# An S5 recurrence run as two halves, each half as two chains side by side, with eight GLU sums opened early

## The chip, the core and the metric

The kernel runs on one core of one Trainium2 chip. The metric is device time in microseconds of one execution. Smaller is faster. The engines named below are TensorE (PE: matmuls, with PEld for its weight loads), VectorE (DVE), ScalarE (ACT), GpSimd (POOL), and SyncE (SP), whose queue issues nearly all DMAs.

## What is computed

The reference runs a sequence of 256 tokens of width 2048 through two attention layers (the first block), and then through a second block, whose mixer is a bidirectional S5 state-space layer with a gated linear unit, followed by a squared-ReLU MLP. Everything is float32. The part that matters here, cut:

```
def s5_scan(u, lam_bar, b_bar, s0, reverse):           # per group of 16 channels, 64 complex states
    bu = einsum('btgh,gph->btgp', u, b_bar)
    bu = bu.at[:, first].add(lam_bar * s0)
    return associative_scan(s[t] = lam_bar * s[t-1] + bu[t])

def s5_mixer(h_ctx, h_lat, ...):                       # 128 groups, both directions
    y = u_lat * d
    for direction in range(2):
        st_lat = s5_scan(u_lat, lam_bar, b_bar, s_ctx_final, reverse)
        y = y + einsum('btgp,ghp->btgh', st_lat, c_mat).real
    z = gelu(y)
    a, g = split(z @ w_glu, 2)                         # w_glu is 2048 x 4096
    return a * sigmoid(g)

def second_block(x, ...):
    x = x + gt1 * rmsnorm(s5_mixer(modulate(rmsnorm(x))))
    x = x + gt2 * rmsnorm(square(relu(modulate(rmsnorm(x)) @ w1)) @ w2)
```

## The kernel before

Activations lie transposed: 16 tiles of 128 features by 256 tokens. Every large product streams its weights from memory as column tiles of 2048 x 128. A column tile comes in two halves of 512 KB (`_split`, DMA on SP's queue into the `raw` pool). ACT casts each half to a rounded high part (L130) and DVE, now and then POOL, subtracts that from it for a low part (L131). `mm_t` then makes 48 matmuls of 128x128 by 128x256 for one column tile: 16 steps of the contraction, each with high by high (L156), high by low (L157) and low by high (L158), into one bank of the PSUM pool `pj`, which has four banks. Beside the stream, small chunks of the modulation vectors' matrix-vector products (`bg`) are worked off. A chunk loads 1 MB (`graw`), and its product is two DVE multiply-adds (L230) or PE matmuls (L215).

The S5 mixer (`s5_mix`) cuts the sequence into 64 chunks of 4 tokens and turns the recurrence into one over 63 chunk borders. The 128 groups are 8 blocks of 16. For each block, inputs are normalised, transposed and multiplied into the chunk increments, which ACT and DVE write into a state tile `S` (L1388). Then `scan` runs 63 steps, each of three instructions: a complex product in one multiply (L1405), and two adds (L1406, L1407). A step needs the result of the step before. For each block there follows an output part. ACT copies the state into `sn`, one half of it reversed (L1458, L1459); PE makes the output `y` from the inputs (L1433) and from `sn` (L1464); GELU follows on ACT, with POOL's (L1484) or DVE's (L1478) multiplications in between; PE transposes (`zt`, L1495); and ACT writes the high part of `z` (L1499) and either a half-scaled copy, from which POOL subtracts (L1502, L1503), or DVE subtracts directly (L1505).

How the blocks are dealt out stands in a few constants. `SEGS = (2, 2, 2, 1, 1)` makes five segments of blocks with a state tile each. Segment 1 (32 groups) is scanned by POOL, the others by DVE. `SCANS = ((0,), (2,), (3, 4))` gives the DVE calls of `scan`, so segment 0 is a single chain of 32 groups, segment 2 another one, and the two last are written side by side. `ORDER` sets the order of the output parts. `POOL_V` says for which blocks POOL does the GELU multiplications. `BG_M` and `BG_B` say how many `bg` chunks are put ahead of the recurrence and behind each output part.

After the eight output parts, the GLU loop walks over 16 column pairs, `pa` and `pg` (32 column tiles, 1536 matmuls). The contraction runs in the order `kts`, in which the blocks are finished. Sums over the features (L363) run beside it, and the row sums (L373) end it. Then comes the MLP.

The order of the instructions on each engine is set by the scheduler of the framework, which plans the program with a timeline of its own. `issue_after` holds an instruction behind another in this order only, without a wait on the chip.

Of the kernel before, what the change touches and what calls it, by code (L numbers as in the profile page):

```python
# [43 lines left out]
NV = len(VEC)  # L44
SEGS = (2, 2, 2, 1, 1)
SCAN_POOL = (1,)
ORDER = (0, 2, 1, 3, 4)
SCANS = ((0,), (2,), (3, 4))
SLOT = (0, 0, 1, 0, 1)
P_START = ("pe",)  # L50
# [21 lines left out]
JOBS = ("m0", "m02", "mk", "m1", "mc", "m12", "m22", "m24", "m25")  # L72
DVE_W = 1
DVE_V = 1
POOL_V = tuple(range(7))
BG_M = 4
BG_B = 2
TL = True
# [28 lines left out]
class K:  # L107
# [40 lines left out]

    def mm_t(self, a, order=range(KT)):

        H, L = self.weights()
        ps = self.pj.tile([128, T], F32, name="pj", tag="pj")
        for kt in order:
            h, l = H[kt // 8][:, kt % 8], L[kt // 8][:, kt % 8]
            aH, aL = a(kt)
            self.nc.tensor.matmul(ps, h, aH, start=kt == order[0], stop=False)  # L156
            self.nc.tensor.matmul(ps, h, aL, start=False, stop=False)  # L157
            self.nc.tensor.matmul(ps, l, aH, start=False, stop=kt == order[-1])  # L158
        return ps
# [535 lines left out]
    def run(self):  # L695
        tc, I = self.tc, self.I
        from contextlib import ExitStack
        with ExitStack() as es:
# [53 lines left out]
            self.stream_init(items)  # L752
            self.limit = 160

# [582 lines left out]
    def s5_mix(self):  # L1337
        nc, V = self.nc, self.V
        v = nc.vector
# [24 lines left out]
        for k, r in enumerate(segs):  # L1364
            for b in r:
# [14 lines left out]
                uc = [self.sq.tile([64, 4, 2, 64], F32, name="uc", tag="sq") for _ in range(2)]  # L1380
                self.to_chunks(us, ub[b % 2], U[:, b], uc, k < DVE_W)
                for q in range(2):
# [4 lines left out]
                    def evac(ri, ps):  # L1387
                        (v.tensor_copy if ri and k < DVE_W else nc.scalar.copy)(  # L1388
                            S[k][:, n0:n0 + 8, ri, 1:64], ps[:, :, 0:63])
# [3 lines left out]

        def scan(e, *ks):

            a = []
            for n, k in enumerate(ks):
                G, g = 16 * len(segs[k]), 16 * segs[k].start
                o = 512 if k in SCAN_POOL else 800 + 240 * SLOT[k]
                a.append((S[k], view(AB, 4 * g, [[4, G], [2, 2], [1, 2]]), G,  # L1400
                          st[:, o:o + 4 * G].rearrange("p (n q r) -> p n q r", q=2, r=2),
                          st[:, o + 4 * G:o + 6 * G].rearrange("p (n r) -> p n r", r=2)))
# [33 lines left out]

        blocks = [b for k in ORDER for b in segs[k]]
        nxt = within(blocks[0])
        self.bg(BG_M)
        for k in SCAN_POOL:  # L1440
            scan(nc.gpsimd, k)
        for n, b in enumerate(blocks):
            k = seg[b]
            r = segs[k]
            for ks in SCANS:
                if b == r.start and k == ks[0]:
                    scan(v, *ks)
            if n == PF_N:
# [40 lines left out]
            if b == r.start:  # L1489
                zR[k] = self.sp.tile([128, 2 * len(r), 2, T], F32R, name=f"z{k}", tag=f"S{k}")  # L1490
            for s in range(2):
                rows = slice(64 * s, 64 * s + 64)
# [36 lines left out]
        for j in range(KT):  # L1529
            pa = self.mm_t(z_, kts)  # L1530
            af = self.tmp("ga")
# [6 lines left out]
            nc.scalar.activation(xq, x[:, j], AF.Square)  # L1538
            pg = self.mm_t(z_, kts)
            t = self.tmp("gg")  # L1540
# [115 lines left out]
def _layout(i):  # L1656
# [36 lines left out]
    o["b_out"] = _cols(a["b_w_out"][0])  # L1693
    o["glu"] = _cols(a["s5_w_glu_2"][0])
    o["mlp_in"] = _cols(a["w_mlp_in_2"][0])
    o["mlp_out"] = np.stack([_cols(a["w_mlp_out_2"][0, q * 2048:(q + 1) * 2048]) for q in range(4)])
# [32 lines left out]
```

## Time and profile before

| | |
|---|---|
| median of 3 runs | 2579.72 us (2577.77 to 2581.68) |
| profiled execution, its time | 2582.58 us |
| its span | 2580.7 us |
| PE busy | 2374.7 us (92%) |
| DVE busy | 1806.7 us (70%) |
| ACT busy | 1255.4 us (49%) |
| POOL busy | 211.5 us (8%) |
| moved by DMA | 644.66 MB |

Matmul durations overlap in the trace, since TensorE pipelines them. The spacing of their starts is what they cost. A busy share over the whole span mixes stages with different limits, so the stages are read one by one: the stretch in which the recurrence runs on DVE, and the GLU behind it, in which PE is busy throughout.

### The profile page before, as it was taken

What the parts mean: (1) busy time and instruction counts of PE and PEld (TensorE: products, weight loads), DVE (VectorE), ACT (ScalarE), POOL (GpSimd) and SP (SyncE); (2) the same over time, 40 slices, a digit from 0 to 9 for tenths busy, and PEclk for the clock granted to TensorE, in tenths of its full rate; (3) what the DMA queues carried; (4) which work ended last, traced back from release to release, by engine and by line L of the source; (5) the groups of instructions that cost most, each with busy time, mean ns of one, the idle gap of its engine ahead of it and who ended that gap; (6) DMA issues with size and microseconds to landing.
All of it is one profiled execution on the core that took longest, in us unless ns stands there. A gap on an engine that the chain in (4) does not pass through costs nothing.

```text
span 2580.7 us, 48360 instructions
## 1 busy us (share of the span) xinstructions
PE 2374.7 (92%) x18950; PEld 2054.5 (80%) x18950; DVE 1806.7 (70%) x3351; ACT 1255.4 (49%) x2178; POOL 211.5 (8%) x432
## 2 busy tenths in 40 slices
PE   5699999999899999999998634999799999999997
PEld 1299999999688888889986424999688888888885
DVE  3287778878775565788877999876765565665655
ACT  1455554454365555766654335544544443443442
POOL 0000000000011110000000754000000000000000
PEclk7599999999889999999998766999899999999998
DMA  9999999878869998888876634897366666666662
GB/s 322 343 341 324 326 323 339 311 259 321 263 237 337 325 334 296 281 269 272 276 237 213 208 108 138 320 316 263 113 188 190 190 190 186 186 187 191 190 185 93
DMA packets 203316, 644.66 MB, mean 250 GB/s; under 512 B 41008, under 2 KB 49456, under 8 KB 202704
## 3 DMA queue, kind: packets, MB, share of 16 engines
q1 hardware_dynamic: 195616, 620.47, 71.7%
q0 software_dynamic: 7472, 21.11, 2.1%
q8 instruction: 148, 2.42, 0.4%
q14 instruction: 80, 0.66, 0.1%
HBM read 613.71 MB, written 25.69 MB: 248 GB/s over the span
## 4 chain that ended last, share of the span: by engine, by line
PE 82%; DVE 11%; DMA 4%; ACT 2%; issue 1%; SPq 0%; DVEq 0%; POOL 0%; ACTq 0%
PE pj L169 18%; PE pj L156 12%; PE pj L157 12%; PE pj L158 12%; PE pj L170 9%; DMA graw<-in_w_mod 3%; PE g L215 3%; DVE scan_t L1406 3%; PE pjv L193 3%; PE pjv L194 2%; DVE scan_t L1405 2%; PE pjv L195 2%; DVE S L1407 2%; PE inc L690 1%; PE st L363 1%
## 5 line engine op out<-in xcount | busy, mean ns | idle before, releaser
L131 DVE TENSOR_TENSOR wl<-w,wh 128x1024 fp32r<-128x1024 f32 x638 | 778.4, 1224 | 471.8 <-ACT wh L130 462.3
L130 ACT CAST wh<-w 128x1024 fp32r<-128x1024 f32 x640 | 665.6, 1048 | 699.6 <-PE pj L169 280.6
L169 PE MATMUL pj<-h,wh 128*128 128x512 f32 x1024 | 363.3, 400 | 6.1 <-DVE h L413 4.3
L169 PE MATMUL pj<-d,wh 128*128 128x512 f32 x1024 | 358.6, 396 | 0.0
L170 PE MATMUL pj<-h,wl 128*128 128x256 f32 x1024 | 287.5, 281 | 1.1 <-DVE wl L131 1.1
L230 DVE SCALAR_TENSOR_TENSOR gacc<-graw,csilu,gacc 128x1024 f32<-128x1024 f32 x207 | 265.1, 1281 | 32.7 <-DMA graw<-in_w_mod 23.3
L170 PE MATMUL pj<-d,wl 128*128 128x256 f32 x1024 | 284.8, 279 | 0.0
L169 PEld LDWEIGHTS pj<-h,wh 128*128 128x128 f32 x1024 | 194.1, 190 | 54.6 <-issue 3.9
L169 PEld LDWEIGHTS pj<-d,wh 128*128 128x128 f32 x1024 | 191.9, 188 | 47.4 <-PE pj L170 1.7
L156 PE MATMUL pj<-hH,wh 128*128 128x256 f32 x768 | 221.4, 289 | 5.4 <-ACT hH L412 4.0
L158 PE MATMUL pj<-hH,wl 128*128 128x256 f32 x768 | 221.3, 289 | 0.5 <-DVE wl L131 0.5
L157 PE MATMUL pj<-hL,wh 128*128 128x256 f32 x768 | 221.0, 288 | 0.0
L215 PE MATMUL g<-graw,czc 128*32 128x256 f32 x1776 | 170.2, 467 | 53.0 <-DMA graw<-in_w_mod 50.0
L170 PEld LDWEIGHTS pj<-h,wl 128*128 128x128 f32 x1024 | 194.8, 190 | 1.5 <-DVE wl L131 1.5
L170 PEld LDWEIGHTS pj<-d,wl 128*128 128x128 f32 x1024 | 192.8, 188 | 0.4
L156 PEld LDWEIGHTS pj<-hH,wh 128*128 128x128 f32 x768 | 148.7, 194 | 9.0 <-ACT hH L412 4.1
L215 PEld LDWEIGHTS g<-graw,czc 128*32 128x32 f32 x1776 | 46.8, 119 | 132.7 <-DMA graw<-in_w_mod 107.9
L158 PEld LDWEIGHTS pj<-hH,wl 128*128 128x128 f32 x768 | 148.5, 194 | 4.5 <-issue 3.7
L157 PEld LDWEIGHTS pj<-hL,wh 128*128 128x128 f32 x768 | 148.7, 194 | 3.8 <-issue 3.7
L158 PE MATMUL pj<-z,wl 128*128 128x256 f32 x512 | 145.6, 285 | 2.9 <-POOL wl L131 2.7
L156 PE MATMUL pj<-z,wh 128*128 128x256 f32 x512 | 147.3, 289 | 1.0 <-ACT wh L130 1.0
L250 POOL TENSOR_TENSOR m<-gs,vecs 128x4 f32<-128x4 f32 x48 | 19.4, 428 | 1567.3 <-ACT gs L247 1567.3
(473 smaller groups left out, 5494.3 us busy)
## 6 DMA issues: line engine op xcount, KB each, us to landing
graw<-in_w_mod SPq DMA_DIRECT2D x384, 512.0 KB, 5.8
w<-in_mlp_in SPq DMA_DIRECT2D x128, 512.0 KB, 4.5
w<-in_mlp_out SPq DMA_DIRECT2D x128, 512.0 KB, 4.3
w<-in_a_in SPq DMA_DIRECT2D x96, 512.0 KB, 6.5
graw<-in_w_kvmod SPq DMA_DIRECT2D x64, 512.0 KB, 6.6
w<-in_b_in SPq DMA_DIRECT2D x64, 512.0 KB, 5.8
w<-in_glu SPq DMA_DIRECT2D x64, 512.0 KB, 5.4
w<-in_a_v SPq DMA_DIRECT2D x32, 512.0 KB, 5.6
```

The costliest lines, as they stand in the source:

```text
L130: nc.scalar.copy(h, src)
L131: (eng or (nc.gpsimd if next(self.spl) else nc.vector)).tensor_sub(l, src, h)
L156: self.nc.tensor.matmul(ps, h, aH, start=kt == order[0], stop=False)
L157: self.nc.tensor.matmul(ps, h, aL, start=False, stop=False)
L158: self.nc.tensor.matmul(ps, l, aH, start=False, stop=kt == order[-1])
L169: self.nc.tensor.matmul(ps, h, view(aH, 0, [[T, 2], [1, T]]), start=kt == order[0], stop=False)
L170: self.nc.tensor.matmul(ps[:, 0], l, aH, start=False, stop=kt == order[-1])
L193: self.nc.tensor.matmul(ps[:, i], aH[:, s], h, start=half == 0 and i == 0 and k == 0, stop=False)
L194: self.nc.tensor.matmul(ps[:, i], aH[:, s], l, start=False, stop=False)
L215: nc.tensor.matmul(st["g"][32 * q:32 * q + 32], self.cz[c][:, ch * 2 + s], raw[s][:, q * 256:q * 256 + 256], start=st["n"] == 0, stop=ch = ...
L230: nc.vector.scalar_tensor_tensor(acc, raw[s], cc, acc, op0=MUL, op1=ADD)
L1406: e.tensor_add(u, t[:, :, 0], s[:, :, :, c + 1])
```

## The change

The recurrence is cut into two halves of four blocks, each with one state tile. Both are scanned on DVE. Each half is written as two chains of 32 groups side by side: two multiplies, two adds, two adds per step. The second half's scan is put behind the first half's in the order. POOL scans nothing any more.

While the second half is scanned, the first eight contraction steps of eight GLU column tiles (`KO_J = 4` pairs, the blocks 0 to 3) are summed with weights that aren't split: one float32 matmul of 128x128 by 128x256 in place of three (`ko`, 64 of them), in the four `pj` banks. Their weights come from a new input `glu0`, a second copy of that part of the GLU matrix made on the host, in eight loads of 512 KB. For these eight column tiles the stream then skips the first half of the weights (`second_only`), with its cast and subtraction, and their `mm_t` makes 24 matmuls in place of 48.

Three constants of the output parts move work between engines: POOL does the GELU multiplications of the first five blocks only (before, seven), and DVE makes half of the `sn` copies of the last three (before, of the last). Of the `bg` chunks, 12 come ahead of the recurrence and none behind the output parts; before, there were 4 and 10. `DVE_W` is now compared with the block and not with the segment, which names the same two blocks.

```diff
-SEGS = (2, 2, 2, 1, 1)
-SCAN_POOL = (1,)
-ORDER = (0, 2, 1, 3, 4)
-SCANS = ((0,), (2,), (3, 4))
+SEGS = (4, 4)
+KO_J = 4
+KO_K = 8
-DVE_W = 1
-DVE_V = 1
-POOL_V = tuple(range(7))
-BG_M = 4
-BG_B = 2
+DVE_W = 2
+DVE_V = 3
+POOL_V = tuple(range(5))
+BG_M = 12
+BG_B = 0
...
         for i in range(2):
+            if i == 0 and j in self.second_only:
+                H.append(None)
+                L.append(None)
+                continue
...
-    def mm_t(self, a, order=range(KT)):
+    def mm_t(self, a, order=range(KT), ps=None, last=True):
...
-        def scan(e, *ks):
+        def scan(k):
             a = []
-            for n, k in enumerate(ks):
-                G, g = 16 * len(segs[k]), 16 * segs[k].start
+            G = 8 * len(segs[k])
+            for h in range(2):
+                g = 16 * segs[k].start + G * h
...
             for c in range(63):
-                for s, ab, G, t, u in a:
-                    e.tensor_mul(t, view(s, c, [[128, G], [64, 2], [0, 2]]), ab)
-                    e.tensor_add(u, t[:, :, 0], s[:, :, :, c + 1])
-                    e.tensor_add(s[:, :, :, c + 1], u, t[:, :, 1])
+                for s, ab, t, u in a:
+                    v.tensor_mul(t, view(s, c, [[128, G], [64, 2], [0, 2]]), ab)
+                for s, ab, t, u in a:
+                    v.tensor_add(u, t[:, :, 0], s[:, :, :, c + 1])
+                for s, ab, t, u in a:
+                    last = v.tensor_add(s[:, :, :, c + 1], u, t[:, :, 1])
...
+        def open_sums(kt, z):
+            w = self.raw.tile([128, 2 * KO_J, 128], F32, name="wko", tag="raw")
+            nc.sync.dma_start(w.rearrange("p j c -> p (j c)"), I["glu0"][kt])
+            for j in range(KO_J):
+                if kt == 0:
+                    ko.append(self.pj.tile([128, 2, T], F32, name="ko", tag="pj"))
+                for i in range(2):
+                    nc.tensor.matmul(ko[j][:, i], w[:, 2 * j + i], z, start=kt == 0 and i == 0, stop=False)
...
+            if n == 0:
+                with self.tc.issue_after(scan(0)):
+                    scan(1)
...
+                    if 2 * b + s < KO_K:
+                        late.append((2 * b + s, zh))
...
+            for kt, zh in late:
+                open_sums(kt, zh)
...
-            pa = self.mm_t(z_, kts)
+            if j < KO_J:
+                pa, pg = [self.mm_t(z_, kts[KO_K:], ko[j][:, i], i == 1) for i in range(2)]
+            else:
+                pa = self.mm_t(z_, kts)
```

How the scheduler places this is shown at three places. In the rows, the number behind a name tells buffers apart, and the lines of the changed kernel are its own (L1415, L1417 and L1419 are the three instructions of a step there).

The first place is DVE where a second chain joins. Before, `S_16015` is segment 0 (blocks 0 and 1) and `S_16017` segment 2 (blocks 4 and 5):

```order
L1405 TENSOR_TENSOR scan_t<-S_16015,scan_t 128x128
L1406 TENSOR_TENSOR scan_t<-scan_t,S_16015 128x64
L1407 TENSOR_TENSOR S_16015<-scan_t 128x64
L1405 TENSOR_TENSOR scan_t<-S_16015,scan_t 128x128
L1406 TENSOR_TENSOR scan_t<-scan_t,S_16017 128x64
L1406 TENSOR_TENSOR scan_t<-scan_t,S_16015 128x64
L1407 TENSOR_TENSOR S_16017<-scan_t 128x64
L1407 TENSOR_TENSOR S_16015<-scan_t 128x64
```

In the changed kernel, where `S_16015` is the first half (blocks 0 to 3), both chains write into it:

```order
L1419 TENSOR_TENSOR S_16015<-scan_t 128x64
L1415 TENSOR_TENSOR scan_t<-S_16015,scan_t 128x128
L1417 TENSOR_TENSOR scan_t<-scan_t,S_16015 128x64
L1419 TENSOR_TENSOR S_16015<-scan_t 128x64
L1415 TENSOR_TENSOR scan_t<-S_16015,scan_t 128x128
L1417 TENSOR_TENSOR scan_t<-scan_t,S_16015 128x64 x2
L1419 TENSOR_TENSOR S_16015<-scan_t 128x64 x2
L1415 TENSOR_TENSOR scan_t<-S_16015,scan_t 128x128 x2
```

Before, the partner was segment 2; now it is the other chain of the first half. It joins after 12 single steps of the first chain, and 12 single steps of the partner are left at the end of the half. Behind them every step of the second half is a pair, so that there are 51 pair steps, 12 single steps and 63 pair steps after the joining. This is the border of the halves on DVE, with `S_16016` the second half:

```order
L1415 TENSOR_TENSOR scan_t<-S_16015,scan_t 128x128
L1417 TENSOR_TENSOR scan_t<-scan_t,S_16015 128x64
L1419 TENSOR_TENSOR S_16015<-scan_t 128x64
L1415 TENSOR_TENSOR scan_t<-S_16016,scan_t 128x128 x2
L1417 TENSOR_TENSOR scan_t<-scan_t,S_16016 128x64 x2
L1419 TENSOR_TENSOR S_16016<-scan_t 128x64 x2
```

No other work of DVE stands between the two halves.

The second place is PE during the recurrence. Before, the last two output parts and the start of the GLU (L156 to L158) read so; `y` is an output sum, `zt` a transpose:

```order
L1464 MATMUL y_17709<-vl,sn 64x4x16 x32
L215 MATMUL g<-graw,czc_156 32x256 x12
L1495 MATMUL zt<-idn,zb 128x64 x8
L1433 MATMUL y_17800<-ml,U 64x4x16 x16
L1495 MATMUL zt<-idn,zb 128x64 x8
L1433 MATMUL y_17890<-ml,U 64x4x16 x16
L1464 MATMUL y_17800<-vl,sn 64x4x16 x32
L1464 MATMUL y_17890<-vl,sn 64x4x16 x32
L156 MATMUL pj<-z_17273,wh_0_18442 128x256
```

In the changed kernel, this is what PE has between the output parts of the first half:

```order
L1487 MATMUL y_17802<-vl,sn 64x4x16 x32
L1461 MATMUL ko<-zh,wko 128x256 x16
L1519 MATMUL zt<-idn,zb 128x64 x8
L1446 MATMUL y_17912<-ml,U 64x4x16 x16
L1487 MATMUL y_17912<-vl,sn 64x4x16 x4
L1461 MATMUL ko<-zh,wko 128x256 x16
L1519 MATMUL zt<-idn,zb 128x64 x8
L1487 MATMUL y_17912<-vl,sn 64x4x16 x20
L1461 MATMUL ko<-zh,wko 128x256 x16
```

The new matmuls stand in groups of 16 (two contraction steps of eight tiles) between the output parts, where the matrix-vector matmuls (L215) stood before.

The third place is DVE where the recurrence ends. Before, one block's output part is left behind it:

```order
L1405 TENSOR_TENSOR scan_t<-S_16019,scan_t 128x64
L1406 TENSOR_TENSOR scan_t<-scan_t,S_16019 128x32
L1407 TENSOR_TENSOR S_16019<-scan_t 128x32
L1459 COPY sn<-S_16019 64x1024 x2
L131 TENSOR_TENSOR wl_0_18604<-w_0_18601,wh_0_18603 128x1024
L131 TENSOR_TENSOR wl_1_18610<-w_1_18607,wh_1_18609 128x1024
L131 TENSOR_TENSOR wl_0_18624<-w_0_18621,wh_0_18623 128x1024
L1478 SCALAR_TENSOR_TENSOR y_18581<-y_18581,y_18461 128x512
```

In the changed kernel, four blocks' output parts are:

```order
L1415 TENSOR_TENSOR scan_t<-S_16016,scan_t 128x128 x2
L1417 TENSOR_TENSOR scan_t<-scan_t,S_16016 128x64 x2
L1419 TENSOR_TENSOR S_16016<-scan_t 128x64 x2
L1482 COPY sn<-S_16016 64x1024 x6
L1501 SCALAR_TENSOR_TENSOR y_18278<-y_18278,y_18132 128x512
L1501 SCALAR_TENSOR_TENSOR zb<-y_18278,y_18132 128x512
L1531 SCALAR_TENSOR_TENSOR z_18195<-zt,z_18195 128x256 x2
L135 TENSOR_TENSOR wl_1_18446<-w_1_18443,wh_1_18445 128x1024
L1501 SCALAR_TENSOR_TENSOR y_18367<-y_18367,y_18223 128x512
```

The `sn` copies and the GELU of three blocks have moved to DVE behind the scan. The ten other `sn` copies of this half, and its evacuations, stand on ACT behind the same point, with five casts (L130 before) among them. On PE, some 30 matmuls of GLU tiles stand ahead of the last transposes.

## Rows read from the trace of the kernel before

**Rows 1.** Windows, us; busy of PE, PEld, DVE, ACT, POOL; PEclk, DMA share, GB/s.

```profile
1539.60:1607.60 68.00, 34.62 (x564) 28.96 (x564) 65.45 (x304) 38.89 (x58) 26.03 (x34) 0.70 0.43 144
...
1612.30:1818.90 206.60, 203.36 (x1653) 187.32 (x1651) 152.27 (x153) 105.28 (x167) 9.48 (x10) 1.00 0.84 291
```

**Rows 2.** Waits over the whole span: total, times and longest, us.

```profile
ACT sn L1458 <- DVE S L1407: 87.0, 4, 53.4
...
POOL scan_t L1406 <- ACT S L1388: 36.0, 1, 36.0
```

**Rows 3.** Timeline of DVE, single chain: start us, duration us, instruction.

```profile
1417.62 0.29 DVE L1405 TENSOR_TENSOR scan_t<-S,scan_t 128x128 f32<-128x128 f32 x1
...
1418.55 0.29 DVE L1405 TENSOR_TENSOR scan_t<-S,scan_t 128x128 f32<-128x128 f32 x1
...
1425.25 0.35 DVE L1407 TENSOR_TENSOR S<-scan_t 128x64 f32<-128x64 f32 x1
```

**Rows 4.** Timeline of DVE, pair steps beside POOL's scan and without it.

```profile
1492.74 0.59 DVE L1407 TENSOR_TENSOR S<-scan_t 128x64 f32<-128x64 f32 x2
...
1494.36 0.59 DVE L1407 TENSOR_TENSOR S<-scan_t 128x64 f32<-128x64 f32 x2
...
1500.27 0.40 DVE L1407 TENSOR_TENSOR S<-scan_t 128x64 f32<-128x64 f32 x2
...
1501.33 0.39 DVE L1407 TENSOR_TENSOR S<-scan_t 128x64 f32<-128x64 f32 x2
```

**Rows 5.** Timelines of DVE and of POOL where POOL does an output part.

```profile
1589.89 0.23 DVE L1405 TENSOR_TENSOR scan_t<-S,scan_t 128x64 f32<-128x64 f32 x1
1590.15 0.22 DVE L1406 TENSOR_TENSOR scan_t<-scan_t,S 128x32 f32<-128x32 f32 x1
...
1590.65 1.23 DVE L1405 TENSOR_TENSOR scan_t<-S,scan_t 128x64 f32<-128x64 f32 x1
...
1594.66 0.67 DVE L1406 TENSOR_TENSOR scan_t<-scan_t,S 128x32 f32<-128x32 f32 x1
...
1590.53 1.26 POOL L1484 TENSOR_TENSOR y<-y,zb 128x512 f32<-128x512 f32 x1 [11.54 <-ACT y L1481]
...
1594.53 1.41 POOL L1503 TENSOR_TENSOR z<-zh,z 128x256 fp32r<-128x256 f32 x2
```

**Rows 6.** Groups of ACT's instructions, 1379 to 1609 us: busy us, mean ns.

```profile
L1458 ACT COPY sn<-S 64x1024 f32<-64x1024 f32 x16 | 16.6, 1045 | 90.9 <-DVE S L1407 87.0 <-POOL S L1407 3.6
...
L1481 ACT ACTIVATE y<-y 128x512 f32<-128x512 f32 x12 | 7.5, 629 | 0.2
...
L1499 ACT ACTIVATE z<-zt 128x256 fp32r<-128x256 f32 x12 | 4.7, 388 | 8.2 <-PE zt L1495 8.2
...
L130 ACT CAST wh<-w 128x1024 fp32r<-128x1024 f32 x2 | 2.1, 1036 | 0.0
```

**Rows 7.** Timeline of ACT: first and last instruction of two blocks' output parts.

```profile
1539.57 1.04 ACT L1458 COPY sn<-S 64x1024 f32<-64x1024 f32 x1 [14.14 <-DVE S L1407]
...
1558.28 0.41 ACT L1502 ACTIVATE zh<-zt 128x256 f32<-128x256 f32 x1
```

**Rows 8.** Windows inside the GLU and just behind it, columns as in Rows 1.

```profile
1630.00:1660.00 30.00, 30.00 (x238) 26.16 (x237) 26.18 (x27) 17.48 (x30) 1.60 (x2) 1.00 0.98 375
1700.00:1760.00 60.00, 60.00 (x504) 56.61 (x503) 45.01 (x45) 29.88 (x48) 1.44 (x2) 1.00 0.92 321
...
1825.00:1835.00 10.00, 6.32 (x21) 5.25 (x21) 8.76 (x23) 5.09 (x11) 0.00 (x0) 0.51 0.00 0
```

**Rows 9.** Timeline of PE: float32 transposes; the GLU's first matmul.

```profile
1389.15 1.92 PE L667 MATMUL o<-idn,u 128*64 128x128 f32 x8 [0.79 <-ACT u L1378]
...
1600.69 0.39 PE L156 MATMUL pj<-z,wh 128*128 128x256 f32 x1
```

**Rows 10.** The page: GLU weight loads (KB, us to landing), and matrix-vector multiply-adds.

```profile
L230 DVE SCALAR_TENSOR_TENSOR gacc<-graw,csilu,gacc 128x1024 f32<-128x1024 f32 x207 | 265.1, 1281 | 32.7 <-DMA graw<-in_w_mod 23.3
...
w<-in_glu SPq DMA_DIRECT2D x64, 512.0 KB, 5.4
```

More of the change, by code (lines that the diff above doesn't have):

```diff
@@ L44 @@
 NV = len(VEC)
-SEGS = (2, 2, 2, 1, 1)
-SCAN_POOL = (1,)
-ORDER = (0, 2, 1, 3, 4)
-SCANS = ((0,), (2,), (3, 4))
-SLOT = (0, 0, 1, 0, 1)
+SEGS = (4, 4)
+KO_J = 4
+KO_K = 8
 P_START = ("pe",)
@@ L147, in weights @@
         return self.ready.pop(j)
-    def mm_t(self, a, order=range(KT)):
+    def mm_t(self, a, order=range(KT), ps=None, last=True):
         H, L = self.weights()
-        ps = self.pj.tile([128, T], F32, name="pj", tag="pj")
+        opened = ps is not None
+        if not opened:
+            ps = self.pj.tile([128, T], F32, name="pj", tag="pj")
         for kt in order:
@@ L155, in mm_t @@
             aH, aL = a(kt)
-            self.nc.tensor.matmul(ps, h, aH, start=kt == order[0], stop=False)
+            self.nc.tensor.matmul(ps, h, aH, start=kt == order[0] and not opened, stop=False)
             self.nc.tensor.matmul(ps, h, aL, start=False, stop=False)
-            self.nc.tensor.matmul(ps, l, aH, start=False, stop=kt == order[-1])
+            self.nc.tensor.matmul(ps, l, aH, start=False, stop=kt == order[-1] and last)
         return ps
@@ L752, in run @@
             self.stream_init(items)
+            g0 = items.index(next(x for x in items if x.tensor is I["glu"].tensor))
+            self.second_only = set(range(g0, g0 + 2 * KO_J))
             self.limit = 160
@@ L1337, in s5_mix @@
     def s5_mix(self):
-        nc, V = self.nc, self.V
+        nc, V, I = self.nc, self.V, self.I
         v = nc.vector
@@ L1380, in s5_mix @@
                 uc = [self.sq.tile([64, 4, 2, 64], F32, name="uc", tag="sq") for _ in range(2)]
-                self.to_chunks(us, ub[b % 2], U[:, b], uc, k < DVE_W)
+                self.to_chunks(us, ub[b % 2], U[:, b], uc, b < DVE_W)
                 for q in range(2):
@@ L1387, in evac @@
                     def evac(ri, ps):
-                        (v.tensor_copy if ri and k < DVE_W else nc.scalar.copy)(
+                        (v.tensor_copy if ri and b < DVE_W else nc.scalar.copy)(
                             S[k][:, n0:n0 + 8, ri, 1:64], ps[:, :, 0:63])
@@ L1392, in s5_mix @@
             nc.scalar.copy(S[k][:, :, :, 0], self.s0[:, 16 * r.start:16 * r.stop])
-        def scan(e, *ks):
+        def scan(k):
             a = []
-            for n, k in enumerate(ks):
-                G, g = 16 * len(segs[k]), 16 * segs[k].start
-                o = 512 if k in SCAN_POOL else 800 + 240 * SLOT[k]
-                a.append((S[k], view(AB, 4 * g, [[4, G], [2, 2], [1, 2]]), G,
+            G = 8 * len(segs[k])
+            for h in range(2):
+                g = 16 * segs[k].start + G * h
+                o = 512 + 384 * k + 192 * h
+                a.append((S[k][:, G * h:G * h + G], view(AB, 4 * g, [[4, G], [2, 2], [1, 2]]),
                           st[:, o:o + 4 * G].rearrange("p (n q r) -> p n q r", q=2, r=2),
@@ L1403, in scan @@
             for c in range(63):
-                for s, ab, G, t, u in a:
-                    e.tensor_mul(t, view(s, c, [[128, G], [64, 2], [0, 2]]), ab)
-                    e.tensor_add(u, t[:, :, 0], s[:, :, :, c + 1])
-                    e.tensor_add(s[:, :, :, c + 1], u, t[:, :, 1])
+                for s, ab, t, u in a:
[4 more added lines that the diff above has]
+                    last = v.tensor_add(s[:, :, :, c + 1], u, t[:, :, 1])
+            return last.ins
         zR = {}
@@ L1435, in within @@
             return vt, y
-        blocks = [b for k in ORDER for b in segs[k]]
+        blocks = [b for r in segs for b in r]
+        ko = []
+        def open_sums(kt, z):
[6 more added lines that the diff above has]
+                    nc.tensor.matmul(ko[j][:, i], w[:, 2 * j + i], z, start=kt == 0 and i == 0, stop=False)
         nxt = within(blocks[0])
         self.bg(BG_M)
-        for k in SCAN_POOL:
-            scan(nc.gpsimd, k)
         for n, b in enumerate(blocks):
@@ L1444, in s5_mix @@
             r = segs[k]
-            for ks in SCANS:
-                if b == r.start and k == ks[0]:
-                    scan(v, *ks)
+            if n == 0:
+                with self.tc.issue_after(scan(0)):
+                    scan(1)
             if n == PF_N:
@@ L1490, in s5_mix @@
                 zR[k] = self.sp.tile([128, 2 * len(r), 2, T], F32R, name=f"z{k}", tag=f"S{k}")
+            late = []
             for s in range(2):
@@ L1538, in s5_mix @@
             nc.scalar.activation(xq, x[:, j], AF.Square)
-            pg = self.mm_t(z_, kts)
+            if j >= KO_J:
+                pg = self.mm_t(z_, kts)
             t = self.tmp("gg")
@@ L1694, in _layout @@
     o["glu"] = _cols(a["s5_w_glu_2"][0])
+    o["glu0"] = a["s5_w_glu_2"][0][:128 * KO_K].reshape(KO_K, 128, 2, 16, 128)[:, :, :, :KO_J].transpose(
+        0, 1, 3, 2, 4).reshape(KO_K, 128, 256 * KO_J)
     o["mlp_in"] = _cols(a["w_mlp_in_2"][0])
```

## The prediction

> **What bounds the kernel now.** I went from the stages to the single instructions. The windows [rows 1] show two stages that the change touches. In the last part of the recurrence, 1539.6 to 1607.6, PE is busy for 34.6 of 68 us and DVE for 65.5: DVE's steps set the pace, and PE has half its time free. In the GLU, 1612.3 to 1818.9, PE is busy for 203.4 of 206.6 us, and DVE (152.3) and ACT (105.3) are not full. So the first stage is worth what DVE's chain gets shorter, the second what PE has less to do. The waits [rows 2] agree: ACT's `sn` copies wait 87.0 us in four pieces for DVE's last step of a chain, and nothing of that length waits for ACT. All prices of steps come from the DVE timeline.
>
> A step of one chain of 32 groups takes 1418.55 - 1417.62 = 0.93 to 0.94 us for three instructions of 0.27 to 0.29 [rows 3]: each waits for the one before. Two chains side by side take 1494.36 - 1492.74 = 1.62 us per pair step while POOL scans, and 1501.33 - 1500.27 = 1.06 us when POOL is still [rows 4]. A pair thus costs little more than a single step, and far less than two (1.88).
>
> **The change, part by part.** (a) *The recurrence.* Up to 1425.2 nothing differs in the order on DVE: the first chain has made 12 single steps then [rows 3], and blocks 2 and 3 have just been written, since POOL's scan of them began there, after its wait of 36.0 us for their evacuation [rows 2]. From there the order of the changed kernel has 51 pair steps, 12 single steps and 63 pair steps, with nothing between the halves. POOL scans no more, so a pair step is priced at the clean 1.06; the contended 1.62 is its upper end. That gives 51 x 1.06 = 54.1, 12 x 0.94 = 11.3 and 63 x 1.06 = 66.8, together 132.2 us.
>
> (b) *POOL's output work beside the second half.* Its four output parts put 8 instructions of L1484 and 8 of L1503 on POOL. Where POOL begins an L1484 of 1.26 us, a DVE instruction takes 1.23 in place of 0.23, which is 1.0 more; beside the pair of L1503 (1.41 for two) one takes 0.67 in place of 0.22, some 0.46 more [rows 5]. 8 x 1.0 + 8 x 0.46 = 11.7 us. The lower end is 0 (POOL's instruction falls into a gap), the upper one the whole of POOL's time, 8 x 1.26 + 8 x 0.71 = 15.8. I take 11.7, what the DVE rows show. The Trainium skill, "SBUF — State Buffer", section "SBUF: two separate sides", says that a DVE instruction with two SBUF inputs and a GpSimd one that reads SBUF exclude each other for a whole instruction; by it the sum would be the upper end, 4 us more. The rows lie below that, since DVE has often begun first.
>
> The scan then ends at 1425.2 + 132.2 + 11.7 = 1569.1, against 1607.6 before: **-38.5 us**.
>
> (c) *The new matmuls.* 64 float32 matmuls of 128x128 by 256 columns don't occur before. Eight float32 transposes of 128 columns take 1.92 us [rows 9], 0.24 each, so 0.48 for 256 columns and 31 us for all; a rounded 256-column matmul takes 60.0 / 504 = 0.119 [rows 8], so 7.6 us is the low end. Either fits: in the 68 us window alone PE has 33 us idle [rows 1], and the second half of the scan lasts 78 us. I cost them at nothing. Without cover they would cost their 31. Their eight loads take 5.4 us each at most [rows 10], 43 us if each waited for the one before, also under 78; they stand in SP's queue ahead of the later `ml`, `vl` and GLU loads, and the four `pj` banks that they hold are wanted next by a GLU tile that follows their release. Zero, upper end 5.4 for one late load.
>
> (d) *The tail.* Before, one block's output part is left when the scan ends, and GLU matmuls resume 1612.3 - 1607.6 = 4.7 us later with work that doesn't need that block. Now four blocks are left, and GLU tiles have only the steps 8 to 15 to sum, all from these blocks. ACT's part of the tail, from the order: 10 `sn` copies, 5 casts, 10 evacuations and 11 GELU instructions. With [rows 6] that is 10 x 1.045 + 5 x 1.036 + 10 x 0.39 + 11 x 0.6 = 26.2 us. I add 2.3 for waits on PE's transposes (8.2 us are spread over 12 in [rows 6], so three or four such waits): 28.5. It costs 28.5 - 4.7 = **+23.8 us**. Low end 24 in all, no wait and hidden casts; high end two pairs of blocks as today, 1539.57 to 1558.69, 19.1 us each [rows 7], 38.2. The six `sn` copies, GELU multiplications and subtractions on DVE run beside ACT's; if ACT did the copies, that would be 6 x 1.045 more.
>
> (e) *The GLU.* Before, the first 12 of its 1536 matmuls run from 1600.69 on [rows 9], ahead of the scan's end, so 1524 remain. Now there are 1536 - 192 = 1344, of which some 30 stand before the last transposes in the order and run inside the tail. 1314 are left, 210 fewer: 210 x 0.119 = **-25.0 us** [rows 8]. The other work in that stage (row sums, gate chunks) stays.
>
> (f) *The clock.* PE runs little in the tail, and behind the GLU, where it is 63% busy, the granted clock is 0.51, the lower level [rows 8]. If the first 30 matmuls run at it, 3.6 us; if not, 0. I take **+2**.
>
> (g) *Edits at nothing.* Eight casts and eight subtractions fewer (ACT and DVE have room in the GLU). 12 chunks ahead of the recurrence and none behind, 14 before: two move into the GLU, four multiply-adds of 1.28 us [rows 10] on a DVE with 54 us idle there [rows 1]; uncovered 5.1.
>
> Sum: -38.5 + 23.8 - 25.0 + 2 = -37.7 us. Profiled: 2582.6 - 37.7 = 2544.9. The profiled execution lies 2.9 above the median of the runs, so the median becomes **2542**. The tail and the skipped matmuls cancel to within 1.2 us; the gain is that of the recurrence.
>
> **The rivals.** *A tail pair by pair.* PE and ACT do blocks 4 and 5 and then 6 and 7 with their waits, as the two-block parts before: 38.2 in place of 28.5, so 9.7 more, **2552**. For: those parts do take 19.1 us each. Against: the order has all `sn` copies first. Chance 0.17.
>
> *Eight light tiles starve.* A tile with 24 matmuls lasts 2.86 us, and asks for one half of weights and one 1 MB chunk, 1.57 MB, 4.2 us at the 375 GB/s of the densest window [rows 8]. Eight such tiles lose 8 x 1.34 = 10.7 us: **2553**. For: that window's DMA share is 0.98 already. Against: the order puts the eight half loads ahead of the chunks' loads on SP's queue. Chance 0.11.
>
> *Slower: pairs don't overlap on DVE.* If the two chains' instructions wait for each other, since both now write into one state tile, a pair step costs 2 x 0.94 = 1.88, and 114 of them cost 0.82 more each: +93.5, **2635**. The change is a loss from a pair step of 1.06 + 37.7 / 114 = 1.39 us on. For: the chains before had a tile each. Against: the measured pairs take 1.06, and even beside POOL's scan 1.62 [rows 4]; the order alternates the two with nothing between. The Trainium skill, "VectorE: DVE Perf Modes", section "The DRAIN you can't avoid", speaks for this rival: the next instruction waits for the pipe to empty, and leaving out semaphores doesn't skip that (though one that isn't held may begin earlier). By it the pair would cost two single steps; [rows 4] of this kernel disagree. Chance 0.05.
>
> *Better.* POOL's work falls into gaps, the tail is 24, the clock is not lost: 11.7 + 4.5 + 2 = 18 less at best, **2524**; half of it, 2533, is nearer. Chance of under 2530: 0.05. Several small costs that leave less than 5.2 us of gain: 0.02.
>
> **How the numbers follow.** The forecast has 0.60. Its own bounds are POOL's 15.8 (+4.1), the clock's 3.6 (+1.6), a late load of 5.4, and on the other side part of the 18: 2533 to 2552. The range takes in the two rivals of 2552 and 2553 with the forecast's own upper costs, and stops short of the others: **2530 to 2560**. What a measurement of this kernel can tell from no change is about 0.2%, 5.2 us. Faster by more: 0.60 + 0.17 + 0.11 + 0.05 = 0.93; within: 0.02; slower: 0.05.
>
> **What would show it.** In the profile of the changed kernel: 1.06 us from one second add of a pair to the same of the next in the second half, with POOL silent; the last step near 1569; DVE instructions stretched to 1.2 us only beside POOL's GELU multiplications; the 64 new matmuls between the transposes of the first four blocks, done before the scan ends; 28 us from the last step to the last high part of `z`; and from there some 182 us to the end of the GLU's matmuls, at a granted clock of 1.00. A pair step of 1.39 or more, PE waiting for weights in the first eight column tiles, or a tail near 38 would make it wrong, each by the amount above.

## The result, and the profile of the changed kernel

The changed kernel takes 2545.97 us (median of four runs, 2543.05 to 2548.22) against 2580.32 us for the kernel before (four runs): a ratio of 0.9867, with a 95% interval of 0.9850 to 0.9884. It is 34 us faster, where 38 were forecast, and its time lies inside the range. Its profiled execution has a span of 2546.4 us, 34.3 less than before.

The span can be cut at four points: the first add of the recurrence on DVE, its last add, the last high part of `z` on ACT, and the start of the row sums that end the GLU. Up to the last add and up to the last high part, the duration of that instruction is counted in. The kernel before differs in the third point: its last high part comes at 1624.0, when the GLU is running again, so there the tail ends where the GLU's matmuls resume, at 1612.3.

| us | before | forecast | changed |
|---|---|---|---|
| first add of the recurrence at | 1413.4 | 1413.4 | 1408.9 |
| recurrence, first add to last | 194.2 | 155.7 | 158.1 |
| from there until the GLU has PE to itself (the tail) | 4.7 | 28.5 | 31.9 |
| GLU, to its row sums | 206.5 | 183.5 | 183.5 |
| behind the GLU, to the end of the span | 761.8 | 761.8 | 764.0 |

These are the three stages in the windows of the changed kernel (columns as in [rows 1]):

```profile
1408.90:1567.00 158.10, 105.62 (x1268) 80.29 (x1266) 155.38 (x758) 61.22 (x119) 23.20 (x30) 0.80 0.57 181
1567.00:1598.90 31.90, 21.39 (x386) 20.17 (x387) 16.12 (x22) 23.63 (x37) 6.87 (x5) 0.72 0.47 149
1598.90:1782.40 183.50, 180.49 (x1448) 163.41 (x1446) 142.33 (x144) 91.80 (x148) 3.86 (x6) 0.99 0.89 312
```

DVE still fills the recurrence (155.4 of 158.1 us), PE still fills the GLU (180.5 of 183.5). Between them lies a stretch that hardly was there before, in which no engine is full: the tail. The waits of ACT answer to [rows 2]:

```profile
ACT sn L1481 <- DVE S L1419: 41.0, 3, 32.1
...
ACT z L1523 <- PE zt L1519: 18.7, 6, 7.6
```

The waits of ACT for a finished chain went from 87.0 to 41.0 us. The timeline of DVE in the changed kernel answers to [rows 3] and [rows 4]: first the pair joining, then the second adds of the last three steps, the last step whole.

```profile
1421.14 0.29 DVE L1415 TENSOR_TENSOR scan_t<-S,scan_t 128x128 f32<-128x128 f32 x1
1421.46 0.45 DVE L1417 TENSOR_TENSOR scan_t<-scan_t,S 128x64 f32<-128x64 f32 x2
...
1564.49 0.40 DVE L1419 TENSOR_TENSOR S<-scan_t 128x64 f32<-128x64 f32 x2
...
1565.55 0.40 DVE L1419 TENSOR_TENSOR S<-scan_t 128x64 f32<-128x64 f32 x2
...
1565.85 0.49 DVE L1415 TENSOR_TENSOR scan_t<-S,scan_t 128x128 f32<-128x128 f32 x2
1566.26 0.44 DVE L1417 TENSOR_TENSOR scan_t<-scan_t,S 128x64 f32<-128x64 f32 x2
1566.61 0.40 DVE L1419 TENSOR_TENSOR S<-scan_t 128x64 f32<-128x64 f32 x2
```

A pair step takes 1.06 us (from one row of L1419 to the next), as read before the change, although both chains now write into one state tile. The tail shows on POOL, DVE, PE and ACT (their timelines, one after the other):

```profile
1575.36 2.52 POOL L135 TENSOR_TENSOR wl<-w,wh 128x1024 fp32r<-128x1024 f32 x1 [30.77 <-issue]
1577.83 1.72 POOL L1507 TENSOR_TENSOR y<-y,zb 128x512 f32<-128x512 f32 x1
1581.72 1.26 POOL L1507 TENSOR_TENSOR zb<-y,zb 128x512 f32<-128x512 f32 x1 [2.17 <-ACT y L1504]
...
1574.97 0.69 DVE L1482 COPY sn<-S 64x1024 f32<-64x1024 f32 x1 [1.01 <-PE y L1487]
1575.99 2.45 DVE L1482 COPY sn<-S 64x1024 f32<-64x1024 f32 x1 [0.32 <-PE y L1487]
...
1583.04 0.77 PE L1519 MATMUL zt<-idn,zb 64*128 64x64 f32 x8 [7.16 <-POOL zb L1507]
...
1598.27 0.66 ACT L1523 ACTIVATE z<-zt 128x256 fp32r<-128x256 f32 x2 [1.39 <-PE zt L1519]
```

PE stands 7.16 us for POOL's second multiplication of block 4, and POOL began that block late, behind a weight subtraction of 2.52 us (L135). While it ran, a copy on DVE took 2.45 us, where the one before it took 0.69. That this is what makes the tail 31.9 us was the obvious reading, and the experiments don't bear it out.

### The profile page after: what moved, and what is told of

It is laid out like the page before. It is cut to its first block, busy times and chain, and to the rows that moved or that the text cites. A ratio compares the mean times of both kernels' runs of the same rounds, so it can differ in the third digit from the quotient of the medians.

```text
span 2546.4 us, 47968 instructions
## 1 busy us (share of the span) xinstructions
PE 2377.1 (93%) x18854; PEld 2051.9 (81%) x18854; DVE 1776.8 (70%) x3360; ACT 1239.5 (49%) x2153; POOL 118.8 (5%) x234
## 4 chain that ended last, share of the span: by engine, by line
PE 84%; DVE 9%; DMA 3%; ACT 2%; issue 1%; SPq 0%; POOL 0%; DVEq 0%; ACTq 0%; POOLq 0%
PE pj L176 18%; PE pj L163 12%; PE pj L164 12%; PE pj L165 12%; PE pj L177 9%; PE g L222 3%; PE pjv L200 3%; DMA graw<-in_w_mod 3%; PE pjv L201 2%; PE pjv L202 2%; DVE scan_t L1415 2%; DVE scan_t L1417 2%; DVE S L1419 2%; PE inc L697 2%; PE st L370 1%
## 5 line engine op out<-in xcount | busy, mean ns | idle before, releaser
L135 DVE TENSOR_TENSOR wl<-w,wh 128x1024 fp32r<-128x1024 f32 x631 | 770.0, 1224 | 465.2 <-ACT wh L134 457.2
L237 DVE SCALAR_TENSOR_TENSOR gacc<-graw,csilu,gacc 128x1024 f32<-128x1024 f32 x211 | 270.2, 1281 | 27.4 <-DMA graw<-in_w_mod 18.6
L163 PE MATMUL pj<-h1H,wh 128*128 128x256 f32 x512 | 147.1, 290 | 0.3 <-ACT ctx_ws L1323 0.2
L164 PE MATMUL pj<-h1L,wh 128*128 128x256 f32 x512 | 146.4, 287 | 0.0
L165 PE MATMUL pj<-h1H,wl 128*128 128x256 f32 x512 | 146.0, 286 | 0.0
```

The source lines that it names most:

```text
L163: self.nc.tensor.matmul(ps, h, aH, start=kt == order[0] and not opened, stop=False)
L237: nc.vector.scalar_tensor_tensor(acc, raw[s], cc, acc, op0=MUL, op1=ADD)
```

## The experiments

**The changed kernel again**, as a measure for the others.

> The changed kernel itself once more, as the measure for the runs beside it: 2543 to 2549 by its four runs so far. If the part behind the GLU (the MLP) takes 764 us in its profile again, that part is slower in this kernel; if 758 to 762 as in the other profiles, the 2 to 5 us were this execution's own.

It took 2546.71 us (2541.08 to 2549.19). Recurrence 158.0, tail 31.9, GLU 183.5: the same to 0.1 us. The first add comes at 1411.4, 2.5 later. Behind the GLU it took 760.1, so the 764.0 above are that execution's own; the twelve profiles of this study lie between 758 and 764 there. Runs of one kernel spread over 8 us, but these three stages repeat to a tenth, and so they are compared below wherever a few us matter.

**Without the early sums.**

```diff
-KO_J = 4
+KO_J = 0
...
-                    if 2 * b + s < KO_K:
+                    if KO_J and 2 * b + s < KO_K:
```

> The changed kernel without the early sums: all 32 GLU column tiles have 48 matmuls again, and the 64 unsplit matmuls with their eight loads are gone. Theory (the early sums are hidden behind the second half's recurrence, and each GLU matmul that they spare is worth its spacing): 192 x 0.119 = 22.8 us more than the changed kernel's 2546, of which up to 24 matmuls (2.9 us) can run before the tail: 2566 to 2569. Rival (the recurrence alone made the gain, and the shortened GLU tiles were limited by loads or casts, so that the spared matmuls gave nothing): 2546. Second rival (the early sums lengthen the recurrence or the tail by as much as they spare): 2546 as well, with the tail shorter than 32 us and the GLU longer by 23.

2565.73 us, 19 to 20 more. These rows are the last high part of `z` on ACT and the row sums on PE:

```profile
1602.59 0.38 ACT L1523 ACTIVATE z<-zt 128x256 fp32r<-128x256 f32 x1
...
1800.53 1.02 PE L380 MATMUL ysum<-sel_y,ysumt 128*128 128x4 f32 x4 [0.46 <-ACT ysumt L377]
```

The recurrence is as long as with the sums (157.6 us), so they cost it nothing. From its end to the row sums it is 233.9 us against 215.4, 18.5 more; 192 matmuls at 0.119 would be 22.8. Of the 4.3 between, 24 matmuls of one GLU tile (2.9) are hidden: they now run from 1574.9 to 1580.8, where PE otherwise waits in the tail. The last 1.4 I did not follow. Both rivals are out.

**The early sums twice.** Each matmul of L1461 is issued a second time; eight GLU tiles get the contribution of the blocks 0 to 3 doubled.

```diff
+                    nc.tensor.matmul(ko[j][:, i], w[:, 2 * j + i], z, start=False, stop=False)
```

> The changed kernel with each of the 64 early matmuls made twice, so that eight GLU tiles get the contribution of the blocks 0 to 3 doubled: 32 us more of TensorE work in the second half of the recurrence. Theory (these matmuls lie in TensorE's idle time beside VectorE's steps, 33 us of it in the second half's 78): 0 to 5 us more, 2546 to 2551, the few us from the output parts that are queued behind them on TensorE. Rival (the early sums aren't covered, they have cost their 32 us or a good part of it in the changed kernel too): 2560 to 2578.

2549.92 us, 3 to 4 more by the medians; by the stages it is 7. The sums keep PE busy for 58.0 us in place of 32.2, so the work added is 26 us and not the 32 expected, and 43.9 of the 58.0 lie ahead of the scan's end. The recurrence's second half with the doubled sums, and its tail:

```profile
1489.00:1564.20 75.20, 54.68 (x440) 47.71 (x440) 75.20 (x378) 17.32 (x32) 14.40 (x19) 0.84 0.28 86
1564.20:1605.20 41.00, 34.31 (x492) 30.89 (x493) 14.48 (x22) 25.57 (x42) 10.04 (x10) 0.93 0.46 152
```

Even so PE has 20 us idle beside DVE's steps. The tail is 9 us longer, since the last of the four blocks was finished only there (its sums begin at 1571.50, behind the scan's end at 1564.2). PE's part of that block, queued behind the doubled sums, was done at 1546.8, which still was in time. What held it is the order on ACT, where the block's last GELU step (L1505 here) stands behind two `sn` copies of the next block, and these wait for the scan's end:

```profile
1564.15 1.04 ACT L1482 COPY sn<-S 64x1024 f32<-64x1024 f32 x1 [13.67 <-DVE S L1419]
1565.20 1.04 ACT L1483 COPY sn<-S 64x1024 f32<-64x1024 f32 x1
1566.27 0.63 ACT L1505 ACTIVATE y<-y 128x512 f32<-128x512 f32 x1
```

The single sums are covered (the run without them shows it too), and what limited the cover here was not PE's idle time, but that an output part got behind the end of the recurrence in another engine's order.

**One wide chain per half.**

```diff
-            G = 8 * len(segs[k])
-            for h in range(2):
+            G = 16 * len(segs[k])
+            for h in range(1):
```

> The changed kernel with each half scanned as one chain of 64 groups in place of two of 32 side by side: half as many instructions, each twice as wide, each waiting for the one before. Theory (side by side, the second chain's instruction fills the time in which the first's result is awaited): from 0.75 us for a step of 16 groups and 0.94 for 32, a step of 64 should take about 1.32, against 1.07 for a pair. The first half then takes 63 x 1.32 = 83 us from 1421 on in place of 67, and the second 83 in place of 67: 33 us more, about 2579, all of the change's gain. Rival (a step costs its elements alone, however it is written): the same 1.07, 2546. Second rival (cost in proportion to the groups): 1.88 a step, 2646.

2570.43 us, 24 more. The timeline of DVE, one step:

```profile
1544.95 0.42 DVE L1415 TENSOR_TENSOR scan_t<-S,scan_t 128x256 f32<-128x256 f32 x1
1545.40 0.38 DVE L1417 TENSOR_TENSOR scan_t<-scan_t,S 128x128 f32<-128x128 f32 x1
1545.82 0.38 DVE L1419 TENSOR_TENSOR S<-scan_t 128x128 f32<-128x128 f32 x1
1546.24 0.42 DVE L1415 TENSOR_TENSOR scan_t<-S,scan_t 128x256 f32<-128x256 f32 x1
```

A wide step takes 1.29 us against 1.06 for a pair, with the same elements. In the wide step each instruction starts 0.03 to 0.04 us after the one before has ended; in a pair the rows of two instructions each (0.49, 0.44 and 0.40 in the last step shown above) add up to 1.33, more than the step. So two independent chains do overlap on DVE. Over the 114 pair steps that is worth 114 x 0.23 = 26 us, most of the change's gain. Another 12 x (1.29 - 0.94) = 4 come from something else: in the changed kernel the first chain makes 12 single steps while blocks 2 and 3 are prepared, for which the wide chain has to wait. The stages say 28.2 from the changed kernel's scan end to this one's. The step of 1.32 that I had extrapolated was too long by 0.03, 4 us over 126 steps.

**GpSimd quiet beside the recurrence.** GELU multiplications and subtractions of all blocks on DVE; the half-scaled copy on ACT stays for the early sums.

```diff
-POOL_V = tuple(range(5))
+POOL_V = ()
...
-                if n in POOL_V:
+                if 2 * b + s < KO_K:
...
-                    nc.gpsimd.tensor_sub(aL, zh, aH)
+                    v.tensor_sub(aL, zh, aH)
```

> The changed kernel with the GELU multiplications and the subtractions for the low parts of all blocks on VectorE, so that GpSimd does no arithmetic beside the recurrence, save one weight subtraction in the tail. Theory (GpSimd's instructions hold VectorE up for most of their length): the recurrence loses some 12 us of stretched instructions and gains 16 instructions, 8 of 0.69 and 8 of 0.38, 8.6 us: 4 less; the tail no longer waits for GpSimd's two multiplications of block 4, 2 to 5 less; 2537 to 2541. Rival (the stretched instructions have another cause, so they stay): the recurrence gets 8.6 longer, 2550 to 2555.

2540.00 us, 6 less. DVE's instructions of the recurrence by line, first in the changed kernel, then in this one (count, busy us, mean ns):

```profile
L1415 DVE TENSOR_TENSOR scan_t<-S,scan_t 128x128 f32<-128x128 f32 x250 | 67.0, 305 | 0.8
L1417 DVE TENSOR_TENSOR scan_t<-scan_t,S 128x64 f32<-128x64 f32 x252 | 59.7, 275 | 0.8
L1419 DVE TENSOR_TENSOR S<-scan_t 128x64 f32<-128x64 f32 x252 | 58.3, 290 | 0.8
```

```profile
L1415 DVE TENSOR_TENSOR scan_t<-S,scan_t 128x128 f32<-128x128 f32 x250 | 63.0, 289 | 0.8
L1417 DVE TENSOR_TENSOR scan_t<-scan_t,S 128x64 f32<-128x64 f32 x252 | 57.2, 264 | 0.8
L1419 DVE TENSOR_TENSOR S<-scan_t 128x64 f32<-128x64 f32 x252 | 52.7, 266 | 0.7
```

The sum of the three rows went from 185.0 to 172.9 us: GpSimd's work beside the recurrence had stretched DVE's instructions by 12.1. With the same work added to DVE, the recurrence is still 4.8 shorter (153.3 us). It is cheaper to add the multiplications to the busy engine than to let the idle one do them here. The tail is 2 us shorter (29.9).

**Block 4 alone off GpSimd.** Its GELU multiplications and its subtractions go to DVE.

```diff
-POOL_V = tuple(range(5))
+POOL_V = tuple(range(4))
```

> The changed kernel with the first block behind the recurrence's end (block 4) taken from GpSimd to VectorE, all else equal. Theory (the tail of 32 us holds 3 to 5 us of TensorE waiting for GpSimd's second multiplication of this block, behind which the other blocks' matmuls are queued): 3 to 5 less, 2541 to 2543. Rival (the tail is the sum of ScalarE's instructions, 26 us, and its waits are spread over the order whoever does the multiplication): 2546, tail still 31 to 32.

2543.14 us. The medians differ by 2.8, but the stages show only 0.6 of it: a tail of 30.8 in place of 31.9 and a GLU of 184.0 in place of 183.5. PE's timeline shows where the rest of the 7.16 us went:

```profile
1579.19 0.70 PE L1519 MATMUL zt<-idn,zb 64*128 64x64 f32 x8 [3.30 <-DVE zb L1501]
1582.08 0.58 PE L163 MATMUL ko<-z,wh 128*128 128x256 f32 x1 [2.19 <-ACT z L1523]
```

DVE's `zb` comes earlier, but a GLU matmul that the scheduler placed ahead of the next blocks' matmuls waits for ACT's `z`. One long wait became two short ones: the rival holds for all but 1 us.

**The weight subtraction off GpSimd.**

```diff
-PF_POOL = 1
+PF_POOL = 0
```

> The changed kernel with the one weight subtraction that GpSimd does in the tail (2.52 us) on VectorE. Theory (a GpSimd instruction that reads SBUF holds VectorE up, whatever VectorE does: a copy there took 2.45 in place of 0.69, and GpSimd's own work on block 4 queued behind the subtraction): the copy is back at 0.69, block 4 leaves GpSimd about 2 us earlier, the tail is 2 to 3 us shorter, 2543 to 2544. Rival (the subtraction's 1.23 us on VectorE delays the copies as much): no change, 2545 to 2547.

2545.91 us, tail 31.5. DVE's last four copies stand in one row, and PE waits for POOL as before:

```profile
1574.22 3.46 DVE L1482 COPY sn<-S 64x1024 f32<-64x1024 f32 x4
...
1580.22 0.77 PE L1519 MATMUL zt<-idn,zb 64*128 64x64 f32 x8 [6.61 <-POOL zb L1507]
```

Three of the four copies take 0.69 us each, but the first takes 1.64, beside POOL's first multiplication of block 4. All four now stand behind the subtraction on DVE, which waits for ACT's cast, and the last ends 13.0 us behind the scan's end, where it was 11.4 before. POOL's first multiplication does start earlier behind the scan's end (8.9 us in place of 10.8), but its second only by 0.5 (14.2 in place of 14.7), since it waits for ACT. So the rival holds: no change, and later copies.

**The recurrence alone, in the kernel before.**

```diff
-SEGS = (2, 2, 2, 1, 1)
-SCAN_POOL = (1,)
-ORDER = (0, 2, 1, 3, 4)
-SCANS = ((0,), (2,), (3, 4))
-SLOT = (0, 0, 1, 0, 1)
+SEGS = (2, 2, 2, 2)
+SCAN_POOL = ()
+ORDER = (0, 1, 2, 3)
+SCANS = ((0, 1), (2, 3))
+SLOT = (0, 1, 0, 1)
```

> The kernel before with the recurrence alone changed: four segments of two blocks, scanned by VectorE as two pairs one after the other; GpSimd scans nothing; no early sums, and the constants of the output parts, GpSimd's multiplications of seven blocks among them, as before. Theory (the recurrence gains some 40 us, and most of it is lost again, since four blocks are left in the tail, done pair by pair at 19 us each, with the GLU waiting): scan's end near 1567, tail 32 to 38 in place of 4.7, GLU as before or up to 3 us less: 2567 to 2573, of which the early sums and the constants make the changed kernel's 2546. Rival (the tail overlaps the GLU as before, so that the whole gain stays): 2540 to 2545. Second rival (GpSimd's seven blocks eat the gain): 2575 to 2582.

2568.91 us: a ratio of 0.9956 (0.9941 to 0.9971) to the kernel before. The stages in its windows:

```profile
1412.80:1572.80 160.00, 84.29 (x1301) 62.18 (x1298) 157.49 (x758) 73.11 (x131) 23.49 (x28) 0.71 0.52 172
1572.80:1604.60 31.80, 22.99 (x295) 21.39 (x296) 10.80 (x11) 23.08 (x40) 14.96 (x13) 0.73 0.53 166
1604.60:1807.00 202.40, 199.40 (x1599) 181.77 (x1597) 145.93 (x145) 98.62 (x154) 4.00 (x6) 1.00 0.84 289
```

The recurrence is 34 us shorter, and 27 of them go into the tail; the GLU gives 4. So the pair steps alone keep 11 us of the change's 34, since they open a tail of 32 us, and in the changed kernel the early sums pay for it (19 to 20 us, by the run without them). The constants make the rest, some 3 us (2568.91 here, 2565.73 without the early sums). Early sums without the pair steps were not run.

**Everything off GpSimd, and four blocks' copies on DVE.** The quiet kernel with `PF_POOL = 0` and `DVE_V = 4`.

> The changed kernel with GpSimd doing no arithmetic at all beside the recurrence and in the tail (GELU multiplications, subtractions of all blocks and the one weight subtraction on VectorE), and half of the state copies of all four last blocks on VectorE. Theory (the gains of a quiet GpSimd add up: 6 us as measured with the multiplications alone, 2 from the copies that no longer stand behind the weight subtraction, 2 from block 4's copies in two engines): 2536 to 2538 against 2546, better than both kernels. Rival (the tail is held by TensorE's and ScalarE's order, so that earlier copies only wait): 2540, as without these two.

2538.45 us, ratio 0.9838 (0.9823 to 0.9853). Recurrence 153.3, tail 29.0: 0.9 us from the two additions, not 4. Mostly the rival.

**And no GLU matmul ahead of the last output matmuls.**

```diff
-                            nc.tensor.matmul(y[64 * s:64 * s + 64, :, 4 * q + i], sn[:, 2 * i + s, e],
+                            ly = nc.tensor.matmul(y[64 * s:64 * s + 64, :, 4 * q + i], sn[:, 2 * i + s, e],
...
-                pa, pg = [self.mm_t(z_, kts[KO_K:], ko[j][:, i], i == 1) for i in range(2)]
+                with self.tc.issue_after(ly.ins):
+                    pa, pg = [self.mm_t(z_, kts[KO_K:], ko[j][:, i], i == 1) for i in range(2)]
```

> The kernel with the quiet GpSimd, the split on VectorE and four blocks' copies on VectorE, and in addition TensorE's order changed: no GLU matmul ahead of the last block's output matmuls. Theory (in the kernels with the multiplications on VectorE the scheduler put one GLU matmul ahead of two blocks' output matmuls, and TensorE stood 2.2 us there until the first z was written; with it gone the tail gets 2 us shorter, from 29 to 27): 2535 to 2538. Rival (the output matmuls behind it wait for the same thing, a free bank, so that nothing moves): tail still 29, 2537 to 2540.

2536.22 us (2535.89 to 2537.18), ratio 0.9827 (0.9813 to 0.9842), the fastest kernel here, but the tail is 29.3 and the rest as in the run above, so the 2 us between these two medians are not shown to be the edit's. PE in the tail:

```profile
1571.36 0.70 PE L1519 MATMUL zt<-idn,zb 64*128 64x64 f32 x8 [2.72 <-DVE zb L1501]
1574.90 1.98 PE L1446 MATMUL y<-ml,U 128*64 128x64 f32 x32 [2.84 <-DVE zb L1501]
```

The stray matmul is gone, and the output matmuls behind it now wait themselves, for DVE's `zb`: the rival again. In the run above PE stood 2.19 us there for the stray matmul, and the output matmuls began 2.84 us behind the transposes; they do so here too. By the code, output sums and transposes share a PSUM pool of four banks (`m`), so a new output sum needs a bank from which a multiplication has read an old one.

## Why the prediction held, point by point

**What bounds.** Right: the wide-chain run changes DVE's steps alone and the quiet run little else, and the end of the kernel follows by what the recurrence lost or gained.

**(a) The recurrence.** The step price holds nearly, and the numbers of steps do. Forecast 155.7 us from first add to last, measured 158.1: the 51 pair steps of the first half take 54.8 us where 54.1 was forecast, and the 12 single and 63 pair steps behind them 91.2 where 89.8 was forecast with GpSimd's work. One statement was wrong: up to the joining of the second chain the order on DVE is not the same. The scheduler also shuffled the preparation of the inputs ahead of it, and the first add comes at 1408.9 in place of 1413.4. Nine profiles of kernels with the changed structure and the same first half have it at 1406.8 to 1411.4, the two with the old structure at 1412.8 and 1413.4, so some 4 us of the gain seem to be from there. I did not trace which instruction of that stretch brings them, and it stays open. The forecast had nothing for them, and in the profiled span they offset most of what the recurrence (2.4) and the tail (3.4) took more than forecast: that the total came out so near is luck in this part.

**(b) GpSimd beside it.** 11.7 forecast, 12.1 measured in the quiet run. The bounds were sound. The upper one, 15.8, for which I had counted GpSimd's instructions whole by the rule of the Trainium skill ("SBUF — State Buffer", section "SBUF: two separate sides"), is 3.7 more than measured. Whether that is the rule, or my use of it, no run here separates.

**(c) The early sums.** Free, as forecast, at the upper of the two prices; this row of the changed kernel shows 32.2 us for the 64 (two records each), 0.50 per matmul:

```profile
L1461 PE MATMUL ko<-zh,wko 128*128 128x256 f32 x128 | 32.2, 413 | 3.2 <-ACT zh L1526 3.2
```

**(d) The tail.** The term that was mis-sized: 28.5 forecast, 31.9 measured. ACT is busy for 23.6 us in it, 2.6 less than the sum made of its instructions, because back to back an instruction starts some 0.1 us before the end of the one ahead of it (a GELU step of 0.60 us at 1573.21, the next at 1573.70). The waits are 8.3 us, where I had put 2.3 from [rows 6]. I took the waits of an output part in mid-recurrence, where ACT has time to fall behind; in the tail ACT waits for PE, and PE for POOL or DVE. The runs with block 4, the subtraction, the copies and the GLU matmul moved show that no single one of these waits is the tail: each edit took at most 2 us off it, and two of them showed the next wait in its place. The rival of a tail pair by pair (38.2) did not come.

**(e), (f) The GLU and the clock.** 206.5 - 25.0 + 2 = 183.5, measured 183.5, but two errors cancel in it, and that is luck. The first is a count. I had 12 GLU matmuls ahead of the scan's end in the kernel before. There were 36, since 24 more run between 1572.96 and 1580.51, in a gap of the recurrence that I had not looked at. The first of them, and one of the three groups of 500 that the GLU stage of the kernel before has left:

```profile
1572.96 0.39 PE L156 MATMUL pj<-z,wh 128*128 128x256 f32 x1 [1.02 <-ACT wh L130]
...
L156 PE MATMUL pj<-z,wh 128*128 128x256 f32 x500 | 143.2, 288 | 0.0
```

So 1500 remained and not 1524. In the changed kernel 33 of 1344 run in the tail (forecast: some 30) and 1311 behind it. The stage lost 189 matmuls and not 210, which is 22.5 us at 0.119 in place of 25.0. The second error is the clock. The granted clock is 0.64 on average in the first 25 us behind the scan and 1.00, the upper level, when the GLU matmuls begin at 1592.16; from the second on these start 0.12 us from one another:

```profile
1592.16 0.39 PE L163 MATMUL ko<-z,wh 128*128 128x256 f32 x1
1592.38 0.28 PE L164 MATMUL ko<-z,wh 128*128 128x256 f32 x1
1592.50 0.28 PE L165 MATMUL ko<-z,wl 128*128 128x256 f32 x1
```

So the clock's 2 us did not occur. The 22.5 agree with the measured 23.0 without them. The eight light tiles did not starve: PE has no wait for a load or a cast between 1592 and 1785.

**The rivals.** The slower side (pairs that don't overlap) is excluded by the 1.06, and the wide-chain run shows how much hangs on it. The two terms that I said cancel, tail and spared matmuls, do so only roughly: 27.2 lost and 23.0 gained.

## What to carry to other kernels

Where an engine works through a chain of dependent instructions, look for a second chain for the same engine before looking for a second engine: here two on DVE cost 1.06 us per step against 0.94 for one, while GpSimd's help beside them made it 1.62. What is saved in a chain turns into a tail when its last consumers come all at once, so it pays to have ready work that doesn't need them, put where another engine has idle time under the chain. In a tail whose engines wait for each other in turn, moving one instruction buys what lies between the longest wait and the next, not its length.

## What the runs showed of the hardware

Two DVE instructions of which neither needs the other's result overlap. The wide step's instructions, each waiting for the one before, have 0.03 to 0.04 us between end and start; the pair's three rows of two take 1.33 us by their durations and 1.06 by their starts. The Trainium skill, "VectorE: DVE Perf Modes", section "The DRAIN you can't avoid", says that the pipe empties between instructions with or without semaphores; these rows disagree with that sentence taken alone, and agree with the same section's remark that an instruction that isn't held starts earlier than that.

Beside a GpSimd instruction that reads SBUF, a DVE instruction with a single input was held up too: the copy of 0.69 us took 2.45 beside GpSimd's subtraction of 2.52, and 1.64 beside a multiplication of 1.70 in the run with that subtraction moved. An add, which has two inputs, took as long at the end of the recurrence in the kernel before with pairs, beside the same subtraction (rows of DVE, then of POOL):

```profile
1570.07 0.27 DVE L1406 TENSOR_TENSOR scan_t<-scan_t,S 128x64 f32<-128x64 f32 x1
1570.37 2.46 DVE L1407 TENSOR_TENSOR S<-scan_t 128x64 f32<-128x64 f32 x1
...
1570.36 2.35 POOL L131 TENSOR_TENSOR wl<-w,wh 128x1024 fp32r<-128x1024 f32 x1 [34.60 <-issue]
```

GpSimd's memsets, which read nothing, don't show in the steps: beside two of them (1.09 us from 1513.12 on) the pair steps of the changed kernel take 1.06 and 1.07 us.
